# FFN of the last two blocks: one ring of four tiles for the rows of w_down and the columns of w_up

## The chip, the core and the metric

One core of one Trainium2 chip runs the whole program. The metric is the device time of one execution in microseconds (us); the median of three runs is compared. The profile is of one further execution, with its own time.

## What is computed

The reference is one decoder block: dilated attention and a spatial gating unit, then a SwiGLU FFN, on 2048 rows of width 1024, all in float32. Only the end of the program matters here, the FFN:

```
D_FF = 2816
h = rms_norm(x, pre_ffn_norm[l])
f = (jax.nn.silu(h @ w_gate[l]) * (h @ w_up[l])) @ w_down[l]
x = x + rms_norm(f, post_ffn_norm[l])
```

The 2048 rows are four blocks of 512 rows. The FFN of blocks 0 and 1 is done block by block; blocks 2 and 3, "the last two blocks", are done together with seven half-size products in place of eight (Strassen's scheme in Winograd's form).

## The kernel before

A float32 operand is split for TensorE (PE) into a high and a low part: ScalarE (ACT) casts it into `w_hi` (L1055), VectorE (DVE) subtracts to get `w_lo` (L1056), and three matmuls hi·hi, hi·lo, lo·hi take the place of one. `split` does this into a ring of W_SPL = 4 pairs, so the cast of a product waits until the product four places earlier has left PE.

**st_up** (L1136 on, named by its matmuls, L1169) runs NG = 11 rounds, g = 0 to 10, one for each 256 columns of `w_gate` and `w_up`. A round has a gate half and an up half. Each half is the seven products in the order PROD = (1, 2, 5, 6, 3, 7, 4), each of 12 matmuls of 128x512 into one PSUM bank, so a half has 84 matmuls and a round 168. For a half:

- `st_raw` loads two tiles of 512 KB with columns of the weight: the gate's into `raw` (a ring of F_RAW = 4, pool `rw`), the up half's into `rau` (a ring of 2, pool `up`). The left operands of products 1, 2 and 4 are pieces of these tiles; those of 5, 6, 3 and 7 are four sums that GpSimd (POOL) makes into `ss` tiles (L1154 to L1157).
- `gain_b` takes each finished bank out of PSUM into the half's four slots A, B, D and E: copies on ACT (L1065, L1069), additions on DVE (L1067 to L1076) and two more on POOL (L1074, L1077). A and E of the gate half lie in `fe` tiles (pool `us`), B and D and all slots of the up half in `fs` tiles (pool `up`).

Once a round the rows of `w_down` of that round, two tiles of 128x1024, are turned into four combinations in place by DVE (L1175 to L1178) and stored to the DRAM tiles `tS` for the last stage. They have a tile of their own, `wd`, with one buffer. At the end of a round come the silu (L1182), the product gate·up (L1183, four times), POOL's sums into `fc` (L1187 to L1190) and seven stores to `fS`.

```
            wr = pool.tile([P, 2, 1024], F32, name="wd", tag="wd", bufs=1)
            for k in range(2):
                self.dma(wr[:, k], t["w_down"][0, 256 * g + P * k:256 * g + P * k + P])
            for n in range(2):
                r = self.raw0 if g == 0 and n == 0 else self.st_raw(g, n, self.rw if n == 0 else pool)
```

Round 0's gate columns, `raw0`, are loaded ahead, while the FFN of block 1 (`ffn_down(1)`) still runs; pool `rw` is open then. Pool `up` takes memory that `ffn_down(1)` still uses: nothing can be written there before the last of its eight stores `out<-y` (each made ready by a DVE row L907, which waits for a load `xr`) has landed.

All DMAs here stand in the queue of SyncE (SP), in one order, as do the instructions of each engine in theirs; a scheduler fixes these orders when the program is built, from priorities and its own estimates. What stands at the head and waits holds what is behind it. The splits have a raised priority (HP_W = 1000), and so have the rows that empty PSUM (HP_E = 1000).

**st_down**, the last stage, multiplies by `w_down` (L1255); it reads `fS` and `tS`.

Of the kernel before, what the change touches and what calls it, by code (L numbers as in the profile page):

```python
# [10 lines left out]
F32 = mybir.dt.float32  # L11
# [7 lines left out]
P = 128  # L19
# [68 lines left out]
F_RAW = 4  # L88
# [12 lines left out]
class Body:  # L101
# [977 lines left out]
    def st_raw(self, g, n, pool):  # L1079

        w = self.t[("w_gate", "w_up")[n]][0].rearrange("(k p) c -> p k c", p=P)
        r = []
        for j in range(2):
            r.append((pool.tile([P, 1024], F32, name="raw", tag="raw", bufs=F_RAW) if n == 0 else
                      pool.tile([P, 1024], F32, name="rau", tag="rau", bufs=2)).rearrange("p (k c) -> p k c", k=4))
            self.dma(r[j], w[:, 4 * j:4 * j + 4, 256 * g:256 * g + 256])
        return r

    def st_first(self):
        self.raw0 = self.st_raw(0, 0, self.rw)  # L1090

    def st_prep(self, pool):

# [45 lines left out]
    def st_up(self, pool, spool):  # L1139

        nc, t, v, q = self.nc, self.t, self.nc.vector, self.nc.gpsimd

        used = 0
        for g in range(NG):
            both = []
            wr = pool.tile([P, 2, 1024], F32, name="wd", tag="wd", bufs=1)
            for k in range(2):
                self.dma(wr[:, k], t["w_down"][0, 256 * g + P * k:256 * g + P * k + P])
            for n in range(2):
                r = self.raw0 if g == 0 and n == 0 else self.st_raw(g, n, self.rw if n == 0 else pool)  # L1150
                a11, a12, a21, a22 = (r[j][:, :, P * i:P * i + P] for i in range(2) for j in range(2))
                s1, s2, s3, s4 = (spool.tile([P, 4, P], F32, name="ss", tag="ss", bufs=F_SUM) for _ in range(4))
                with self.tc.high_priority(HP_W):
                    q.tensor_tensor(s1, a21, a22, ALU.add)  # L1154
                    q.tensor_tensor(s2, s1, a11, ALU.subtract)
                    q.tensor_tensor(s4, a12, s2, ALU.subtract)
                    q.tensor_tensor(s3, a11, a21, ALU.subtract)  # L1157
                left = {1: a11, 2: a12, 3: s4, 4: a22, 5: s1, 6: s2, 7: s3}
                slots = [spool.tile([P, TB], F32, name="fe", tag="fe", bufs=2) if n == 0 and j in (0, 3) else
                         pool.tile([P, TB], F32, name="fs", tag="fs", bufs=F_OUT) for j in range(4)]  # L1160
                for i in PROD:
                    hi, lo = self.split(left[i])
                    ps = self.psf[used >= 4 and used % 2].tile([P, 512], F32, name="d", tag="d")
                    used += 1
                    for k in range(4):
                        c = slice(k * P, k * P + P)
                        h, l = self.th[i][k]
                        for n, (a, b) in enumerate(((hi, h), (hi, l), (lo, h))):
                            nc.tensor.matmul(ps, a[:, c], b, start=(k == 0 and n == 0), stop=(k == 3 and n == 2))  # L1169
                    self.gain_b(i, ps, lambda n: slots[n])  # L1170
                    yield
                both.append(slots)
                if len(both) == 1:
                    b11, b12, b21, b22 = (wr[:, i, 512 * j:512 * j + 512] for i in range(2) for j in range(2))
                    v.tensor_tensor(b11, b12, b11, ALU.subtract)  # L1175
                    v.tensor_tensor(b12, b22, b12, ALU.subtract)
                    v.tensor_tensor(b22, b22, b11, ALU.subtract)
                    v.tensor_tensor(b21, b21, b22, ALU.subtract)  # L1178
                    for i, b in ((5, b11), (7, b12), (6, b22), (4, b21)):
                        self.dma(self.tS[i][g], b)  # L1180
            for gt, up in zip(*both):
                nc.scalar.activation(gt, gt, AF.Silu)  # L1182
                v.tensor_tensor(up, gt, up, ALU.mult)  # L1183

            a12, a22, a21, a11 = both[1]
            s1, s2, s4 = (pool.tile([P, TB], F32, name="fc", tag="fc", bufs=F_CMB) for _ in range(3))
            q.tensor_tensor(s1, a21, a22, ALU.add)  # L1187
            q.tensor_tensor(s2, s1, a11, ALU.subtract)
            q.tensor_tensor(s4, a12, s2, ALU.subtract)
            q.tensor_tensor(a21, a11, a21, ALU.subtract)  # L1190
            for i, a in ((1, a11), (2, a12), (5, s1), (6, s2), (3, s4), (7, a21), (4, a22)):
                self.dma(self.fS[i][g], a)
            yield
# [235 lines left out]
```

## Time and profile before

| | us |
|---|---|
| median of 3 runs (2467.46 to 2468.42) | 2468.33 |
| the profiled execution, its own time | 2461.28 |
| its span, first to last instruction | 2459.2 |
| PE busy in the span | 2276.9 (93%) |
| DVE, ACT, POOL busy | 1770.4, 1167.9, 358.5 |
| st_up, from its first matmul to its last | 1759.3 to 2230.4 |

The mean granted clock of PE is 0.968 of full speed. Times in the rows count from the span's start; a row of a timeline gives start, duration, engine, line and operation, and in brackets how long the engine was idle before it and what ended that. Starts of pipelined instructions overlap the end of those before.

### The profile page before, as it was taken

Reading aid. Unit: us, or ns where it says so; the run is one execution under the profiler, and the core shown is the slowest. Engines: PE = TensorE matmul, PEld = TensorE weight load, DVE = VectorE, ACT = ScalarE, POOL = GpSimd, SP = SyncE. Lnnn points to the kernel's source line nnn. Section 1 sums busy time; section 2 is a strip of 40 time slices with the busy share of each in tenths; the row PEclk is TensorE's granted clock in tenths of the full one; section 3 lists DMA queues with packets and bytes.
Section 4 is the critical chain, followed back from the end, with each engine's and each line's share of the span. In section 5 each row is a group of like instructions: output and inputs, shape, how many; then the busy total and the mean of one; then the engine's idle time right before and its main releaser. Section 6 shows DMA issues by size and latency. Waiting matters only on the chain. (4 is left out here: it accounts for less than half of the span.)

```text
span 2459.2 us, 32809 instructions
## 1 busy us (share of the span) xinstructions
PE 2276.9 (93%) x10421; PEld 1859.5 (76%) x10421; DVE 1770.4 (72%) x3430; ACT 1167.9 (47%) x2141; POOL 358.5 (15%) x389
## 2 busy tenths in 40 slices
PE   7998869889888899999999999999979999999997
PEld 6776757677676778887777888788757778887886
DVE  5426887986798995868999744668767676675567
ACT  7425765655645653535555533545423233334543
POOL 0001000000000000000000000000054566561012
PEclk9998989999999999999999999999989999999999
DMA  7868667778777655457665435778466533326655
GB/s 243 296 206 270 210 200 220 226 228 239 249 223 233 197 158 153 137 145 228 202 191 160 135 116 166 226 232 263 147 211 225 199 112 108 103 99 227 199 177 197
DMA packets 346748, 476.84 MB, mean 194 GB/s; under 512 B 30768, under 2 KB 174672, under 8 KB 346064
## 3 DMA queue, kind: packets, MB, share of 16 engines
q1 hardware_dynamic: 345296, 470.57, 60.8%
q0 software_dynamic: 1280, 4.20, 0.5%
q8 instruction: 82, 1.34, 0.2%
q14 instruction: 90, 0.74, 0.1%
HBM read 365.12 MB, written 109.52 MB: 193 GB/s over the span
## 5 line engine op out<-in xcount | busy, mean ns | idle before, releaser
L180 DVE TENSOR_TENSOR w_lo<-w_raw,w_hi 128x512 fp32r<-128x512 f32 x368 | 251.8, 687 | 176.9 <-ACT w_hi L179 163.8
L179 ACT CAST w_hi<-w_raw 128x512 fp32r<-128x512 f32 x368 | 227.4, 619 | 314.4 <-PE d L208 241.9
L208 PE MATMUL d<-ah,w_hi 128*128 128x512 f32 x704 | 276.9, 394 | 4.9 <-ACT ah L334 4.9
L208 PE MATMUL d<-al,w_hi 128*128 128x512 f32 x704 | 276.1, 392 | 0.0
L208 PE MATMUL d<-ah,w_lo 128*128 128x512 f32 x704 | 275.5, 391 | 0.0
L1169 PE MATMUL d<-th,w_lo 128*128 128x512 f32 x616 | 246.9, 401 | 20.3 <-DVE w_lo L1056 20.2
L1169 PE MATMUL d<-th,w_hi 128*128 128x512 f32 x616 | 246.7, 400 | 12.7 <-ACT w_hi L1055 12.7
L1169 PE MATMUL d<-tl,w_hi 128*128 128x512 f32 x616 | 244.1, 396 | 0.0
L1056 DVE TENSOR_TENSOR w_lo<-raw,w_hi 128x512 fp32r<-128x512 f32 x187 | 142.6, 801 | 69.4 <-ACT w_hi L1055 67.9
L1055 ACT CAST w_hi<-raw 128x512 fp32r<-128x512 f32 x187 | 106.9, 618 | 133.0 <-PE d L1255 80.4
L208 PE MATMUL d<-w_hi,hh 128*128 128x512 f32 x384 | 155.7, 408 | 8.8 <-DVE io L445 4.5
L208 PE MATMUL d<-w_lo,hh 128*128 128x512 f32 x384 | 156.9, 409 | 4.3 <-DVE w_lo L180 4.3
L1169 PEld LDWEIGHTS d<-th,w_lo 128*128 128x128 f32 x616 | 118.0, 192 | 52.7 <-DVE w_lo L1056 25.9
L208 PEld LDWEIGHTS d<-ah,w_hi 128*128 128x128 f32 x704 | 133.0, 189 | 30.6 <-ACT ah L334 5.2
L208 PE MATMUL d<-w_hi,hl 128*128 128x512 f32 x384 | 154.9, 405 | 0.0
L827 POOL MEMSET ph<- 128x128 f32 x64 | 13.2, 206 | 953.8 <-PE pv L805 531.9
L208 PEld LDWEIGHTS d<-al,w_hi 128*128 128x128 f32 x704 | 132.7, 188 | 25.6
L208 PEld LDWEIGHTS d<-ah,w_lo 128*128 128x128 f32 x704 | 132.4, 188 | 25.8
L1169 PEld LDWEIGHTS d<-th,w_hi 128*128 128x128 f32 x616 | 118.6, 193 | 38.5 <-ACT w_hi L1055 14.0
L208 PE MATMUL d<-w_hi,fh 128*128 128x512 f32 x352 | 139.7, 397 | 1.5 <-ACT fh L1022 1.1
L208 PE MATMUL d<-w_hi,fl 128*128 128x512 f32 x352 | 137.3, 392 | 2.1 <-DVE fl L1023 2.1
L1169 PEld LDWEIGHTS d<-tl,w_hi 128*128 128x128 f32 x616 | 118.4, 192 | 26.1
(285 smaller groups left out, 5606.4 us busy)
## 6 DMA issues: line engine op xcount, KB each, us to landing
w_raw<-in_w_in SPq DMA_DIRECT2D x136, 256.0 KB
w_lo<-wc SPq DMA_DIRECT2D x96, 256.0 KB
w_raw<-in_w_gate SPq DMA_DIRECT2D x88, 256.0 KB
w_raw<-in_w_up SPq DMA_DIRECT2D x88, 256.0 KB
w_raw<-in_w_down SPq DMA_DIRECT2D x88, 256.0 KB
araw<-fD SPq DMA_DIRECT2D x88, 256.0 KB
raw<-fS SPq DMA_DIRECT2D x77, 256.0 KB
w_raw<-in_w_out SPq DMA_DIRECT2D x64, 256.0 KB
```

The costliest lines, as they stand in the source:

```text
L179: nc.scalar.copy(hv, rv)
L180: nc.vector.tensor_tensor(lv, rv, hv.bitcast(F32), ALU.subtract)
L208: nc.tensor.matmul(banks[b], lhsT, rhs, start=(k == 0 and j == 0), stop=(k == nk - 1 and j == len(ops) - 1))
L827: nc.gpsimd.memset(t[:, :o].bitcast(F32), 0.0)
L1055: nc.scalar.copy(hv, src)
L1056: nc.vector.tensor_tensor(lv, src, hv.bitcast(F32), ALU.subtract)
L1169: nc.tensor.matmul(ps, a[:, c], b, start=(k == 0 and n == 0), stop=(k == 3 and n == 2))
```

## The change

The up half's columns and the rows of `w_down` now share one ring of four tiles `rau`, in place of two `rau` and one `wd` of double size: the memory is the same. In round 0 and in odd rounds `w_down` is asked for first, in the other rounds the columns of `w_up`. `st_first` now loads the up columns of round 0 ahead as well; they go into the two `raw` tiles in which, before, the gate columns of round 1 were loaded ahead.

```diff
         r = []
+        tag, bufs = ("raw", F_RAW) if pool is self.rw else ("rau", 4)
         for j in range(2):
-            r.append((pool.tile([P, 1024], F32, name="raw", tag="raw", bufs=F_RAW) if n == 0 else
-                      pool.tile([P, 1024], F32, name="rau", tag="rau", bufs=2)).rearrange("p (k c) -> p k c", k=4))
+            r.append(pool.tile([P, 1024], F32, name=tag, tag=tag, bufs=bufs).rearrange("p (k c) -> p k c", k=4))
             self.dma(r[j], w[:, 4 * j:4 * j + 4, 256 * g:256 * g + 256])
         return r
 
     def st_first(self):
-        self.raw0 = self.st_raw(0, 0, self.rw)
+        self.raw0 = [self.st_raw(0, n, self.rw) for n in range(2)]
...
+        def down(g):
+            w = [pool.tile([P, 1024], F32, name="rau", tag="rau", bufs=4) for _ in range(2)]
+            for k in range(2):
+                self.dma(w[k], t["w_down"][0, 256 * g + P * k:256 * g + P * k + P])
+            return w
+
         used = 0
         for g in range(NG):
             both = []
-            wr = pool.tile([P, 2, 1024], F32, name="wd", tag="wd", bufs=1)
-            for k in range(2):
-                self.dma(wr[:, k], t["w_down"][0, 256 * g + P * k:256 * g + P * k + P])
+            if g == 0:
+                wr, raws = down(g), self.raw0
+            elif g % 2:
+                wr, raws = down(g), [self.st_raw(g, 0, self.rw), self.st_raw(g, 1, pool)]
+            else:
+                raws = [self.st_raw(g, n, p) for n, p in enumerate((self.rw, pool))]
+                wr = down(g)
             for n in range(2):
-                r = self.raw0 if g == 0 and n == 0 else self.st_raw(g, n, self.rw if n == 0 else pool)
+                r = raws[n]
...
-                    b11, b12, b21, b22 = (wr[:, i, 512 * j:512 * j + 512] for i in range(2) for j in range(2))
+                    b11, b12, b21, b22 = (wr[i][:, 512 * j:512 * j + 512] for i in range(2) for j in range(2))
```

The four combinations of `w_down` are L1187 to L1190 in the changed file, its silu L1194, its gate·up L1195.

The scheduler orders the program anew. First place: ACT at the end of round 0's gate half. `raw` and `rau` are weight columns, `ss` POOL's sums, `fs<-d` with L1069 is the copy of slot B out of PSUM. Before:

```order
L1055 CAST w_hi<-raw 128x512
L1069 COPY fs<-d 128x512
L1182 ACTIVATE fs<-fs 128x512 x2
L1182 ACTIVATE fe<-fe 128x512
L1055 CAST w_hi<-rau 128x512 x2
L1055 CAST w_hi<-ss 128x512 x3
```

With the change:

```order
L1055 CAST w_hi<-raw 128x512 x3
L1055 CAST w_hi<-ss 128x512 x3
L1069 COPY fs<-d 128x512
L1065 COPY fs<-d 128x512
L1055 CAST w_hi<-ss 128x512
L1194 ACTIVATE fs<-fs 128x512 x2
```

Five casts of the up half (two of its columns, three of its sums) now stand ahead of the copy that needs pool `up`; before, all seven stood behind it.

Second place: DVE at the start of round 2's gate half. `w_lo<-ss` are the low parts of products 5, 6, 3 and 7, `w_lo<-raw` that of product 4; `wd<-wd` and `rau<-rau` are combinations of `w_down`. Before:

```order
L1183 TENSOR_TENSOR fs<-fs 128x512
L1175 TENSOR_TENSOR wd<-wd 128x512
L1071 TENSOR_TENSOR fs<-d,fs 128x512
L1056 TENSOR_TENSOR w_lo<-ss,w_hi 128x512
L1183 TENSOR_TENSOR fs<-fe,fs 128x512
L1176 TENSOR_TENSOR wd<-wd 128x512
L1177 TENSOR_TENSOR wd<-wd 128x512
L1056 TENSOR_TENSOR w_lo<-ss,w_hi 128x512
L1178 TENSOR_TENSOR wd<-wd 128x512
L1067 TENSOR_TENSOR fe<-d,fe 128x512
```

With the change:

```order
L1195 TENSOR_TENSOR fs<-fe,fs 128x512
L1187 TENSOR_TENSOR rau<-rau 128x512
L1056 TENSOR_TENSOR w_lo<-ss,w_hi 128x512
L1067 TENSOR_TENSOR fe<-d,fe 128x512
L1056 TENSOR_TENSOR w_lo<-ss,w_hi 128x512
L1188 TENSOR_TENSOR rau<-rau 128x512
L1189 TENSOR_TENSOR rau<-rau 128x512
L1056 TENSOR_TENSOR w_lo<-raw,w_hi 128x512
L1190 TENSOR_TENSOR rau<-rau 128x512
```

Of the four combinations one is left ahead of the low part of product 3, and two stand ahead of that of product 4. The even blocks of `w_down` are combined in the up halves instead, and the gate half of round 3 has none.

Third place: SP at the same point of the changed program, with the numbers of the tiles; `tS5_3` is combination 5 of block 3 of `w_down`, `fS3_1` a store of round 1.

```order
L139 DMA tS4_2_274<-rau_18647 128x512
L139 DMA rau_18960<-in_w_down 128x1024
L139 DMA fS4_1_185<-fs_18485 128x512
L139 DMA fS5_1_196<-fc_18624 128x512
L139 DMA fS6_1_207<-fc_18625 128x512
L139 DMA fS7_1_218<-fs_18486 128x512
L139 DMA fS2_1_163<-fs_18484 128x512
L139 DMA fS3_1_174<-fc_18626 128x512
L139 DMA rau_18961<-in_w_down 128x1024
L139 DMA tS5_3_286<-rau_18960 128x512
```

Block 3's second tile of `w_down` is asked for behind the last store of round 1. Before, the queue at this store was ahead with `w_down`:

```order
L139 DMA wd_19599<-in_w_down 128x1024 x2
L139 DMA tS5_5_288<-wd_19599 128x512
L139 DMA fS4_1_185<-fs_18483 128x512
L139 DMA fS5_1_196<-fc_18622 128x512
L139 DMA fS6_1_207<-fc_18623 128x512
```

There the combinations of block 5 were stored ahead of round 1's results; now block 3 follows them.

## Rows read from the trace of the kernel before

**Rows 1.** Stretches: from:to, length, each engine's busy us (instructions), PE's clock, DMA share, GB/s.
```profile
1759.30:1817.10 57.80, 43.08 (x169) 33.87 (x168) 40.92 (x59) 15.57 (x27) 20.07 (x14) 0.85 0.52 173
1817.10:2003.10 186.00, 167.72 (x689) 133.32 (x689) 132.20 (x153) 51.01 (x91) 104.69 (x69) 0.95 0.56 192
2003.10:2230.40 227.30, 227.30 (x995) 186.51 (x994) 151.06 (x168) 75.41 (x131) 134.31 (x89) 1.00 0.31 100
```

**Rows 2.** Waits of PE in st_up: total us, times, the longest.
```profile
PE d L1169 <- DVE w_lo L1056: 20.2, 11, 3.7
PE d L1169 <- ACT w_hi L1055: 12.7, 3, 11.6
```

**Rows 3.** Timeline of PE, round 0, gate half to up half.
```profile
1783.84 0.40 PE L1169 MATMUL d<-th,w_lo 128*128 128x512 f32 x1
1795.84 0.79 PE L1169 MATMUL d<-th,w_hi 128*128 128x512 f32 x1 [11.61 <-ACT w_hi L1055]
1796.44 0.63 PE L1169 MATMUL d<-tl,w_hi 128*128 128x512 f32 x1
...
1800.44 0.40 PE L1169 MATMUL d<-th,w_lo 128*128 128x512 f32 x1
```

**Rows 4.** Timeline of ACT, round 0.
```profile
1788.98 0.59 ACT L1069 COPY fs<-d 128x512 f32<-128x512 f32 x1 [15.03 <-DMA out<-y]
...
1795.17 0.62 ACT L1055 CAST w_hi<-rau 128x512 fp32r<-128x512 f32 x1 [1.41 <-DMA rau<-in_w_up]
...
1808.89 0.62 ACT L1055 CAST w_hi<-raw 128x512 fp32r<-128x512 f32 x1 [1.64 <-PE d L1169]
```

**Rows 5.** Timeline of DVE, round 0: the last two rows L907.
```profile
1783.46 0.75 DVE L907 SCALAR_TENSOR_TENSOR y<-y,po_y,xr 128x512 f32<-128x512 f32 x1 [1.41 <-DMA xr<-x]
1785.93 0.75 DVE L907 SCALAR_TENSOR_TENSOR y<-y,po_y,xr 128x512 f32<-128x512 f32 x1 [1.71 <-DMA xr<-x]
```

**Rows 6.** Timeline of SP's queue, round 0.
```profile
1779.67 7.37 SPq L139 DMA_DIRECT2D out<-y  x4
1788.93 0.81 SPq L139 DMA_DIRECT2D wd<-in_w_down  x2
```

**Rows 7.** Timeline of DVE, gate half of round 2.
```profile
1877.13 1.78 DVE L1177 TENSOR_TENSOR wd<-wd 128x512 f32<-128x512 f32 x1
...
1880.50 1.75 DVE L1056 TENSOR_TENSOR w_lo<-ss,w_hi 128x512 fp32r<-128x512 f32 x1
```

**Rows 8.** Timeline of PE, gate half of round 2.
```profile
1882.30 0.79 PE L1169 MATMUL d<-th,w_lo 128*128 128x512 f32 x1 [3.71 <-DVE w_lo L1056]
```

**Rows 9.** Timeline of SP's queue: the first store fS of two rounds, five rounds apart.
```profile
2003.15 0.34 SPq L139 DMA_DIRECT2D fS<-fs  x1
...
2195.36 0.33 SPq L139 DMA_DIRECT2D fS<-fs  x1
```

**Rows 10.** Timeline of ACT: cast for the gate half's first product, a late round.
```profile
2029.78 0.62 ACT L1055 CAST w_hi<-raw 128x512 fp32r<-128x512 f32 x1 [1.58 <-PE d L1169]
```

**Rows 11.** Timeline of DVE in that gate half: low parts of products 3 and 7.
```profile
2045.00 1.79 DVE L1056 TENSOR_TENSOR w_lo<-ss,w_hi 128x512 fp32r<-128x512 f32 x1
...
2047.31 1.18 DVE L1056 TENSOR_TENSOR w_lo<-ss,w_hi 128x512 fp32r<-128x512 f32 x1
```

**Rows 12.** Timeline of POOL in that gate half.
```profile
2047.90 1.75 POOL L1189 TENSOR_TENSOR fc<-fs,fc 128x512 f32<-128x512 f32 x1
...
2051.43 1.63 POOL L1155 TENSOR_TENSOR ss<-ss,raw 128x512 f32<-128x512 f32 x1
```

**Rows 13.** Timeline of SP's queue in that gate half: last store fS of a round.
```profile
2049.67 0.32 SPq L139 DMA_DIRECT2D fS<-fc  x1
2050.22 0.38 SPq L139 DMA_DIRECT2D raw<-in_w_gate  x1
```

**Rows 14.** Timelines of SP's queue and DVE: a load of w_down and its first reader.
```profile
1947.63 0.81 SPq L139 DMA_DIRECT2D wd<-in_w_down  x2
...
1951.38 0.69 DVE L1175 TENSOR_TENSOR wd<-wd 128x512 f32<-128x512 f32 x1 [0.42 <-DMA wd<-in_w_down]
```

## The prediction

> **What bounds the kernel now.** I looked first at where st_up, the only stage touched, runs below its own best rate. The stretches [rows 1] show three parts: from 2003.1 us on PE is busy all the time at full clock; from 1817.1 to 2003.1 it is busy 167.7 of 186.0 us at a mean clock of 0.95; in round 0, the first 57.8 us, only 43.1 at 0.85. So the last part gives the price of an undisturbed round: five rounds lie between two like stores [rows 9], (2195.36 - 2003.15) / 5 = 38.44 us, which is 2.75 for each of the 14 products. Against that, the stage loses time in its first five rounds alone.
>
> Then the waits of PE [rows 2]: 32.9 us, all on ACT's casts or DVE's low parts; no load of weights is a releaser directly. I split the loss by place.
>
> *Round 0.* The gate half's last matmul starts at 1783.84 and the next at 1795.84 [rows 3]. ACT shows why [rows 4]: it stood 15.03 us at the copy of slot B, in pool `up`, until the last store `out<-y` had landed at 1788.9; the cast of the up columns behind it then waited until 1795.17 for a load that SP could only issue behind those same stores [rows 6]. The cast at 1808.89 [rows 4] was released by the end of the up half's fourth product (the ring of four pairs); three products more give the end of round 0: 1808.89 + 3 x 2.75 = 1817.1. The up half thus took 1817.1 - 1784.1 = 33.0 us in place of 19.2.
>
> *Rounds 1 to 10.* They end at 2230.4 [rows 1], so they took 413.3 us; ten undisturbed ones take 384.4. The loss is 28.9 us, in the four boundaries between rounds 0 and 4, 7.2 each. One of them is shown: DVE does combinations of `w_down` at 1.78 us a row [rows 7], the low part of product 3 comes behind them, and PE waits 3.71 us for it [rows 8]. These boundaries lose because the scheduler lets `w_down` run far ahead: its eleven blocks are done in the first five rounds, as the third place of the order shows.
>
> **The change, part by part.**
>
> *(a) Round 0, the up half.* Its columns are in SBUF long before, and POOL's four sums follow the gate's at once. Product 1 starts where the gate half ends, 1784.1. Product 2 can't: PSUM banks are taken in turn, and its bank is the one that held the gate half's third product, slot B, whose copy still waits for the last `out<-y`. The stores depend on the same L907 rows as before [rows 5]; the low parts that now stand between them fall into DVE's waits for `xr` (1.71 and 1.41 us idle [rows 5], 0.7 a row). New on SP is one gate tile of 512 KB just ahead of the last store. Its buffer is free by then, so it does not block the queue, but its packets do go first: nothing at best, and at worst its own landing, which I bound by the 3.75 us of a 512 KB load (below). Stores and loads overlap, so I take 0.6: the store lands at 1789.5, the copy takes 0.6 [rows 4], product 2 starts at 1790.1. PE has then been idle about 3.3 us and comes back at half clock: before, after its pause, nine matmuls came 0.427 apart in place of 0.228 [rows 3], a price of 1.8 us. Six products: 1790.1 + 6 x 2.75 + 1.8 = 1808.4. **Gain: 1817.1 - 1808.4 = 8.7 us** (5.5 to 9.3 by the bounds).
>
> *(b) `w_down` no longer runs ahead.* With tiles freed only by up columns, block 2 waits for round 1's up half, block 4 for round 3's, and each odd block for the even one before it. Even blocks are combined in up halves, where DVE has idle time; odd ones at the next gate half's start. At the boundary of rounds 0 and 1 the combinations (block 1) stand ahead of POOL's additions, whose results DVE would wait for anyway: I cost them at nothing. The cover is DVE's wait for POOL; without it they cost 4 x 1.78 at most, of which three products of slack (8.2 us) take all. So the loss of rounds 1 to 10 goes, **28.9 us**, but for what follows.
>
> *(c) The odd blocks 3, 5, 7 and 9: a new wait.* Take a late gate half as a clock: the cast for product 1 is released at 2029.78 [rows 10], so product 1 starts three products later, 2038.0, and product 4, the seventh, at 2054.5; its third matmul wants the low part at 2054.95. On DVE one combination (1.78 [rows 7]) now comes before the low part of product 3: that moves from 2046.8 to 2048.5 [rows 11]; PE wants it at 2049.4, so it costs nothing, with 0.9 to spare. Then DVE meets the second combination, which needs block 3's second tile. SP issues that behind the round's last `fS` store; this waits for POOL until 2049.65 [rows 12], and the next load starts at 2050.22 [rows 13]. From issue to first reader a load of this shape took 1951.38 - 1947.63 = 3.75 us [rows 14]. So DVE goes on at 2053.95; two combinations and the low part of product 4 at 0.69 each (a row that meets no POOL work [rows 14]) end at 2056.0, and PE waits 1.05 us. POOL has ended its second sum at 2053.1 [rows 12], and its next row waits for one that stands behind on DVE. Behind DVE's wait are also the low parts for the up half, wanted from 2058 on; they follow in 2 to 3 us. Four boundaries: **loss 4.2 us**.
>
> Here a row bears against me: a combination took 0.69 us [rows 14] in one place and 1.78 in another [rows 7], and a low part 1.75, where POOL was at work. With these, (c) ends at 2053.95 + 2 x 1.78 + 1.75 = 2059.3, a wait of 4.3 us, which also brings the half clock, as after 3.71 us [rows 8], 1.8 more: 24 us in place of 4.2. The Trainium skill has this as a rule (SBUF — State Buffer, Who interferes with whom): GpSimd and a DVE row with two SBUF inputs exclude each other on a shared port pair, and the later one waits. By this rule alone, were POOL busy there, the sum would be the 24. The trace agrees with it on the two durations; it does not say that POOL is at work at that moment, and I take 0.69.
>
> *(d) At nothing.* Gate columns of round 1 now arrive later, with the loads that round 2's had, at 1785, and are wanted at 1800. Later up columns come about a round ahead of use. SP's waits for tiles hold `fS` stores for a few us; no reader wants those before st_down. Bytes, matmuls and the stages before and after are the same.
>
> **The sum.** 8.7 + 28.9 - 4.2 = 33.4 us. The profiled execution would go from 2461.28 to 2427.9. It was 7.05 below the median of the runs, and a gain in waits should carry over: 2468.33 - 33.4 = **2434.9 us**. Its own range: 2428, with (a) at its best, no half clock after the pause (1.8) and no wait in (c); 2445, with (a) at 5.5 and 0.7 us more at each of ten boundaries.
>
> **The rivals.**
>
> 1. *POOL is at work in (c).* The 24 us of above: gain 8.7 + 28.9 - 24 = 13.6, **2454.7**; with two of the three rows slowed, about 2447. For it: a slip of 2 us in POOL's order suffices. Against it: POOL's next row depends on DVE.
> 2. *The stalls move to the odd boundaries.* Each costs what each of the four cost, 7.2 us. Four of them: only (a) is left, **2459.6**; with that of round 0 to 1 as a fifth, gain 1.5, **2466.8**, no change. For it: the same rows remain on the same engine. Against: there were four combinations and the wait for POOL in one place, now two or three.
> 3. *Slower: one combination chain in every round.* Were `w_down` in the way at all ten boundaries at 7.2 us, the loss would be 72: 2468.33 - 37.6 + 72 = **2502.7**. It turns slower when a boundary costs over 37.6 / 10 = 3.8 us. The place would be the low parts of products 3 and 4, the price DVE held by a late tile. For it: a late tile on an in-order engine did hold DVE before. Against: the order leaves the even boundaries without such rows, so odd ones would have to cost over 9 us.
> 4. *The ring does not change places.* It does only in part: block 3 goes into the tiles of block 2, not of the up columns. What I cost is the order as built, so this gives no other time.
>
> **How the numbers follow.** Forecast 0.66, rival 1 0.18 (half of it below 2452), rival 2 0.09 (0.06 and 0.03), rival 3 0.05, nothing seen 0.02. The range 2427 to 2453 takes the forecast and over half of rival 1, and leaves out some 0.2. A measurement of this kernel tells 0.2%, 4.9 us, from no change. Faster by more: 0.66 + 0.18 + 0.06 = 0.90; within: 0.05; slower: 0.05.
>
> **What would show it.** (a) PE: a pause of about 3 us after the twelfth matmul of round 0's up half, ended by the copy of slot B; end of round 0 near 1808. (b) No waits of PE at the boundaries into rounds 1, 2 by more than 2 us and into 3, 5 at all, and full clock from 1815 on. (c) DVE waiting for `rau<-in_w_down` at the second combination of odd blocks, and PE for `w_lo` about 1 us, four times. The forecast is wrong if these four waits are 4 us, if PE waits 2 us or more in even rounds, or if the last `out<-y` lands after 1792.

## The result and the profile after

Four executions of the changed kernel took 2435.27 to 2442.55 us, median 2439.82; four of the kernel before, on the same chip, had a median of 2468.38. The ratio is 0.9882, 95% interval 0.9860 to 0.9905. The forecast was 2434.9, in a range of 2427 to 2453, and faster with a chance of 0.90; the median lies in the range, 4.9 us above the forecast. The parts of the sum came out otherwise than forecast. The profiled execution took 2438.17 us (span 2435.2), and its `st_up` is 25 us shorter, not 33.

What follows goes by the length of `st_up` and its halves: from the first matmul of a half (84 matmuls) to that of the next, in PE's timeline. An undisturbed half is 19.23 us, a round 38.45.

| | `st_up` starts | round 0 | rounds 1 to 10 | `st_up` |
|---|---|---|---|---|
| before | 1759.29 | 57.87 | 413.15 | 471.02 |
| after | 1759.69 | 44.97 | 400.85 | 445.82 |

The stretches of the changed kernel, one line each, with the columns of [rows 1]: round 0; round 1 and the gate half of round 2; up to the gate half of round 8; the rest.

```profile
1759.70:1804.66 44.96, 41.82 (x169) 33.28 (x168) 36.91 (x56) 15.34 (x28) 22.21 (x15) 0.92 0.51 173
1804.66:1874.43 69.77, 61.34 (x254) 48.60 (x252) 48.82 (x54) 17.28 (x31) 41.79 (x28) 0.95 0.56 186
1874.43:2109.38 234.95, 231.57 (x1009) 189.19 (x1008) 169.04 (x193) 75.73 (x132) 147.68 (x96) 1.00 0.47 155
2109.38:2205.51 96.13, 96.13 (x421) 78.92 (x420) 65.41 (x77) 32.98 (x58) 52.26 (x34) 1.00 0.35 118
```

Only the last stretch, five halves of 19.23, is undisturbed. The second should take three such halves, 57.7, and takes 69.8. So of the 28.7 us that rounds 1 to 10 lost before, 16.3 are still lost: 0.35 in the gate half of round 1, 7.39 in its up half (26.62), 4.34 in the gate half of round 2 (23.57), and 1.11, 1.00 and 2.11 in the gate halves of rounds 4, 6 and 8 (20.34, 20.23, 21.34). These are the waits of PE in `st_up`, the answer to [rows 2]; below them DVE's waits for `w_down`, first with the change, then before.

```profile
PE d L1181 <- DVE w_lo L1056: 11.2, 7, 2.1
PE d L1181 <- ACT w_hi L1055: 3.7, 3, 2.6
```

```profile
DVE rau L1188 <- DMA rau<-in_w_down: 22.6, 9, 5.2
...
DVE rau L1187 <- DMA rau<-in_w_down: 17.2, 5, 10.2
```

```profile
DVE wd L1175 <- DMA wd<-in_w_down: 12.7, 6, 3.7
...
DVE wd L1176 <- DMA wd<-in_w_down: 4.2, 4, 2.1
```

PE waits 14.9 us in place of 32.9. DVE, though, stands 39.8 us at combinations (L1187, L1188) whose tile of `w_down` has not landed, in place of 16.9 before. Runs 5 to 7 test how much of what remains comes from these combinations.

*Round 0.* The forecast had PE stop at the second product of the up half until slot B was copied. PE's timeline at the start of the first product and of the fourth:

```profile
1785.21 0.39 PE L1181 MATMUL d<-th,w_lo 128*128 128x512 f32 x1
1785.43 0.39 PE L1181 MATMUL d<-th,w_hi 128*128 128x512 f32 x1
...
1793.67 0.39 PE L1181 MATMUL d<-th,w_hi 128*128 128x512 f32 x1
```

Nothing stops: three products in 8.24 us, 2.75 each, and the half takes 19.23. Yet the copy was even later than forecast (ACT's timeline, then SP's queue):

```profile
1792.62 0.59 ACT L1069 COPY fs<-d 128x512 f32<-128x512 f32 x1 [3.79 <-DMA out<-y]
```

```profile
1783.54 3.60 SPq L139 DMA_DIRECT2D out<-y  x3
1787.24 0.39 SPq L139 DMA_DIRECT2D raw<-in_w_gate  x1
1788.51 0.33 SPq L139 DMA_DIRECT2D out<-y  x1
```

The last store was issued at 1788.51 and landed at 1792.6, not 1789.5; the copy ended at 1793.2. PE did not care: the second product ran before the copy, so slot B's bank is not its bank. The bank goes to the fourth product, which starts at 1793.67, half a microsecond after the copy; in runs 3, 4 and 7 PE does wait for this copy, and at the fourth product each time. Why the banks are given out in this order, no run shows. The same place before is in [rows 3, 4, 6].

*Rounds 1 and 2.* PE's waits there, and DVE in the up half of round 1:

```profile
1832.54 0.50 PE L1181 MATMUL d<-th,w_hi 128*128 128x512 f32 x1 [2.64 <-ACT w_hi L1055]
...
1835.23 0.79 PE L1181 MATMUL d<-th,w_lo 128*128 128x512 f32 x1 [1.96 <-DVE w_lo L1056]
...
1864.14 0.50 PE L1181 MATMUL d<-th,w_lo 128*128 128x512 f32 x1 [1.67 <-DVE w_lo L1056]
...
1872.02 0.50 PE L1181 MATMUL d<-th,w_lo 128*128 128x512 f32 x1 [2.11 <-DVE w_lo L1056]
```

```profile
1833.29 0.69 DVE L1187 TENSOR_TENSOR rau<-rau 128x512 f32<-128x512 f32 x1 [10.20 <-DMA rau<-in_w_down]
1833.89 0.68 DVE L1076 TENSOR_TENSOR fe<-d,fe 128x512 f32<-128x512 f32 x1
1834.49 0.68 DVE L1056 TENSOR_TENSOR w_lo<-ss,w_hi 128x512 fp32r<-128x512 f32 x1
```

DVE stands 10.20 us at the first combination of block 2. Behind it is the low part that PE wants: PE waits 1.96, and ten matmuls follow 0.43 apart (a granted clock of 0.50, the 1.2 GHz level). PE's wait before that, 2.64, is another: it ended at 1832.54, before DVE's did, with a cast of ACT (1831.88) that stood behind a silu. Both waits and the slow matmuls come to 7.4 us. The silu on ACT, and POOL:

```profile
1831.35 0.63 ACT L1194 ACTIVATE fs<-fs 128x512 f32<-128x512 f32 x1 [11.78 <-POOL fs L1074]
```

```profile
1822.50 1.74 POOL L1169 TENSOR_TENSOR ss<-rau 128x512 f32<-128x512 f32 x1
...
1827.43 1.30 POOL L1166 TENSOR_TENSOR ss<-raw 128x512 f32<-128x512 f32 x1 [3.20 <-issue]
```

The silu waits for POOL's L1074 (1830.05), and POOL does that row behind its sums of round 2's gate columns, which it begins only at 1827.43. The trace does not name what ended that wait, but the second of the two tiles of columns was issued 4.7 us earlier, at 1822.74, and in runs 5 and 10 POOL begins there 4.7 and 4.9 us after the same load. SP had stood until 1820.8 at a store `fS` of POOL's L1201; the load heads these rows of SP:

```profile
1822.74 0.51 SPq L139 DMA_DIRECT2D raw<-in_w_gate  x1
1823.30 2.48 SPq L139 DMA_DIRECT2D rau<-in_w_up  x2
1825.88 0.45 SPq L139 DMA_DIRECT2D raw<-in_w_gate  x1
1826.43 0.44 SPq L139 DMA_DIRECT2D rau<-in_w_down  x1
```

Before, when round 0's up columns took none of the `raw` tiles, the same tile was issued at 1774.70. The tile of `w_down` is late by POOL and SP too: block 2 goes into a tile of round 1's up columns, and POOL's last sum reads that until 1824.24. SP reaches the load at 1826.43, behind four others, and it lands at 1833.3, 6.9 us later.

*A later boundary* (gate half of round 4), on DVE, SP, POOL and PE:

```profile
1938.57 1.78 DVE L1187 TENSOR_TENSOR rau<-rau 128x512 f32<-128x512 f32 x1
1940.28 1.78 DVE L1056 TENSOR_TENSOR w_lo<-ss,w_hi 128x512 fp32r<-128x512 f32 x1
...
1947.97 0.69 DVE L1188 TENSOR_TENSOR rau<-rau 128x512 f32<-128x512 f32 x1 [4.21 <-DMA rau<-in_w_down]
1948.70 0.69 DVE L1189 TENSOR_TENSOR rau<-rau 128x512 f32<-128x512 f32 x1
1949.31 0.68 DVE L1056 TENSOR_TENSOR w_lo<-raw,w_hi 128x512 fp32r<-128x512 f32 x1
```

```profile
1943.24 0.32 SPq L139 DMA_DIRECT2D fS<-fc  x1
1943.61 0.42 SPq L139 DMA_DIRECT2D rau<-in_w_down  x1
```

```profile
1938.06 1.75 POOL L1202 TENSOR_TENSOR fs<-fs 128x512 f32<-128x512 f32 x1
...
1945.01 1.29 POOL L1167 TENSOR_TENSOR ss<-ss,raw 128x512 f32<-128x512 f32 x1
1952.53 1.63 POOL L1074 TENSOR_TENSOR fs<-fs 128x512 f32<-128x512 f32 x1 [6.23 <-DVE fs L1073]
```

```profile
1950.05 0.50 PE L1181 MATMUL d<-th,w_lo 128*128 128x512 f32 x1 [0.84 <-DVE w_lo L1056]
```

This is step (c) as it was forecast, row by row: the second tile issued behind the last `fS` store, DVE at L1188 until it lands (4.4 us after its issue), POOL with nothing to do from 1946.3 to 1952.5, combinations and low part at 0.69, and PE waiting 0.84 where 1.05 was forecast.

### The profile page after: what moved, and what is told of

Its sections match the earlier page's. It is cut to its first block, busy times and chain, and to the rows that moved or that the text cites. A ratio compares the mean times of both kernels' runs of the same rounds, so it can differ in the third digit from the quotient of the medians.

```text
span 2435.2 us, 32794 instructions
## 1 busy us (share of the span) xinstructions
PE 2268.8 (93%) x10421; PEld 1857.9 (76%) x10421; DVE 1766.2 (73%) x3430; ACT 1168.5 (48%) x2141; POOL 364.3 (15%) x389
## 5 line engine op out<-in xcount | busy, mean ns | idle before, releaser
L1181 PEld LDWEIGHTS d<-th,w_lo 128*128 128x128 f32 x616 | 117.0, 190 | 39.5 <-DVE w_lo L1056 14.6
L208 PE MATMUL d<-w_lo,fh 128*128 128x512 f32 x352 | 137.5, 391 | 0.0
```

Source lines behind the costliest of these rows:

```text
L208: nc.tensor.matmul(banks[b], lhsT, rhs, start=(k == 0 and j == 0), stop=(k == nk - 1 and j == len(ops) - 1))
```

## The experiments

Every kernel ran beside the kernel before on one chip; the ratio is to that kernel's runs beside it. Lengths of `st_up` are taken as above.

### 1. Only the early load

The kernel before, with:

```diff
-            r.append((pool.tile([P, 1024], F32, name="raw", tag="raw", bufs=F_RAW) if n == 0 else
+            r.append((pool.tile([P, 1024], F32, name="raw", tag="raw", bufs=F_RAW) if pool is self.rw else
...
-        self.raw0 = self.st_raw(0, 0, self.rw)
+        self.raw0 = [self.st_raw(0, n, self.rw) for n in range(2)]
...
-                r = self.raw0 if g == 0 and n == 0 else self.st_raw(g, n, self.rw if n == 0 else pool)
+                r = self.raw0[n] if g == 0 else self.st_raw(g, n, self.rw if n == 0 else pool)
```

> Only the early load of round 0's up columns; w_down keeps its own single tile and the up columns their two, as before. My theory (the two parts add): round 0 takes 45.0 us as in the changed kernel in place of 57.9, PE has no pause at the start of its up half, and rounds 1 to 10 keep a loss of about 29 us, since w_down runs ahead as before. Time about 12.9 below the kernel before, 2455. Rival A (the parts don't add): with round 0 shorter the same rows of w_down are squeezed into fewer rounds, the loss of rounds 1 to 10 grows to 35 or more, and the gain is under 7, 2462 or more. Rival B (the ring gives nothing): the early load alone gives all, 2440.

Measured: 2460.21 us, ratio 0.9963 (0.9946 to 0.9980). Round 0 took 44.88 us, rounds 1 to 10 420.15; `st_up` is 6.0 shorter than before. Rival A holds by the stage (the median is 2 us under its number): the early load gives its 13 us in round 0 and gives back 7.0 in rounds 1 to 10, where the loss is now 35.7. Their gate halves of rounds 1 to 4 take 26.64, 29.19, 27.57 and 28.61.

### 2. Only the ring

The changed kernel, with:

```diff
-        self.raw0 = [self.st_raw(0, n, self.rw) for n in range(2)]
+        self.raw0 = self.st_raw(0, 0, self.rw)
...
-                wr, raws = down(g), self.raw0
+                raws = [self.raw0, self.st_raw(g, 1, pool)]
+                wr = down(g)
```

> Only the ring: round 0's up columns are not loaded ahead, they take two tiles of the ring first, and w_down of block 0 the other two. My theory (the two parts add): PE pauses 10 to 12 us between the halves of round 0, which takes 57 to 58 us as before, and rounds 1 to 10 lose 12 to 17 us in place of 29, most of it in the up half of round 1 and the gate half of round 2. Gain 11 to 16, 2452 to 2457. Rival: the ring's own loss in rounds 1 and 2 comes from round 0 being short; with the pause back it goes, rounds 1 to 10 lose only the 4 us of the odd blocks, gain about 25, 2443.

Measured: 2449.21 us, ratio 0.9922 (0.9896 to 0.9947). The two stretches of this kernel, round 0 and rounds 1 to 10:

```profile
1777.71:1835.11 57.40, 43.82 (x170) 34.09 (x168) 41.05 (x56) 15.46 (x27) 20.88 (x14) 0.85 0.48 163
1835.11:2232.38 397.27, 388.42 (x1682) 315.76 (x1680) 285.76 (x323) 125.83 (x221) 242.63 (x158) 1.00 0.45 149
```

My theory held for the stage's numbers: the pause of round 0 is back (10.28 us), rounds 1 to 10 lose 12.8, and `st_up` is 16.4 shorter than before. The median is 3 us under its range. The place was a miss: the up half of round 1 takes 19.23 and loses nothing, and the loss is in the gate halves of rounds 1 and 2 (24.25 and 23.27). So the 7.4 us of the changed kernel's up half came with the early load, as the rival had it, and others came in their stead. The parts don't simply add: 6.0 + 16.4 = 22.4, both together 25.2. The early load costs 7.0 us of new waits without the ring, and 3.6 with it (400.85 - 397.27).

### 3. Round 1 takes its up columns first

```diff
-            elif g % 2:
+            elif g % 2 and g > 1:
```

> The changed kernel, but round 1 takes its up columns from the ring before w_down of block 1. In the changed kernel DVE stood 10.20 us at the first combination of block 2, PE lost 7.4 us in the up half of round 1 and 4.3 in the gate half of round 2. My theory (a chain in the ring: up columns of round 1 wait for the stores of block 0, POOL's sums wait for these columns, block 2 is loaded into tiles that POOL frees, and DVE stands in order behind it): with the columns first, POOL's sums of round 1's up half end before 1820 in place of 1824.2, DVE's wait for block 2 falls under 5 us and PE's loss in that half under 2.5; time 5 to 9 below the changed kernel, 2431 to 2435. Rival (DVE and POOL slow each other, whatever the ring does): the sums still end after 1822, the wait stays at 8 to 11 us, time within 2 of the changed kernel.

Measured: 2445.63 us, ratio 0.9902 (0.9870 to 0.9935); `st_up` 446.57. The mechanism was right where I looked: POOL's sums of round 1's up half ended 59.5 us after the stage's start in place of 64.6, DVE's wait for block 2 fell from 10.20 to 6.29 (more than expected still), and the up half of round 1 took 19.23. The length of the stage was the rival's, 0.8 us from the changed kernel (the medians are 5.8 apart, with intervals that overlap), for another reason: the gate half of round 1 now took 26.41, that of round 2 24.91. DVE and PE in the gate half of round 1:

```profile
1824.04 1.78 DVE L1188 TENSOR_TENSOR rau<-rau 128x512 f32<-128x512 f32 x1
1825.86 1.63 DVE L1189 TENSOR_TENSOR rau<-rau 128x512 f32<-128x512 f32 x1
1827.41 1.75 DVE L1056 TENSOR_TENSOR w_lo<-ss,w_hi 128x512 fp32r<-128x512 f32 x1
```

```profile
1822.48 0.50 PE L1181 MATMUL d<-th,w_lo 128*128 128x512 f32 x1 [1.49 <-DVE w_lo L1056]
...
1829.21 0.79 PE L1181 MATMUL d<-th,w_lo 128*128 128x512 f32 x1 [3.70 <-DVE w_lo L1056]
```

Block 1's combinations now stand among the low parts of the gate half, with POOL at work: 26.41 - 19.23 = 7.2 us, the price of a boundary in the kernel before, with its 3.71 us wait [rows 7, 8].

### 4. Every round takes its up columns first

```diff
-            elif g % 2:
+            elif g < 0:
```

> The changed kernel, but every round after round 0 takes the up columns first and w_down second, odd rounds too. My theory: as in the run before this one for rounds 1 and 2, and the waits of DVE for the second tile of blocks 3, 5, 7 and 9 (4.0 to 5.2 us each, issued behind the last store fS3) go to places where a half round of slack lies ahead; PE's waits of 0.84, 0.71 and 1.83 us in the gate halves of rounds 4, 6 and 8 go as well. Another 4 to 8 below the run before, 2424 to 2430. Rival 1: a block of w_down is then late in every round, as block 2 was in the changed kernel, PE loses 2 us or more in each of eight rounds, and the time is 2450 or more. Rival 2: nothing but the place of the waits changes, within 2 of the run before.

Measured: 2442.0 us, ratio 0.9888 (0.9865 to 0.9912); `st_up` 447.75. A miss: the gate half of round 1 lost 8.6 us, and the gate halves of rounds 3 to 10 all lose something now, 0.9 to 2.2 us each. By the stage it is rival 2, 1.2 us from run 3; the medians are 3.6 apart, with intervals that overlap. Asking for tiles in another order moves the late combination; it does not remove it.

### 5. No combinations

```diff
-                    v.tensor_tensor(b11, b12, b11, ALU.subtract)
-                    v.tensor_tensor(b12, b22, b12, ALU.subtract)
-                    v.tensor_tensor(b22, b22, b11, ALU.subtract)
-                    v.tensor_tensor(b21, b21, b22, ALU.subtract)
```

> The changed kernel without the 44 combinations of w_down on DVE: the blocks are stored as they were loaded. The loads, the ring and the stores stay. My theory (what is left of the loss in the changed kernel, 16.3 us in rounds 1 to 10, is DVE standing at a combination for a late tile, and combinations standing between low parts): rounds 1 to 10 take 384.5 to 387, each gate half 19.2, the up half of round 1 as well; st_up takes 430 to 432 in place of 445.8. Rival (the loss comes from POOL's sums and the loads of the columns, DVE only waits with the rest): the up half of round 1 still takes over 23 us and rounds 1 to 10 over 394.

Measured, one execution: 2431.48 us, `st_up` 430.99, rounds 1 to 10 386.68. From round 1 on all gate halves take 19.2, as my theory has it; the up half of round 1 is still longer than it says, 21.37. So 14.2 of the 16.3 us hang on the combinations, with loads, stores and ring in place; 2.1 are the other chain of round 1, from the late gate tile over POOL and ACT: PE waits 1.53 us there, for ACT's cast.

### 6. Odd blocks combined in their own round

`self.low` is the low part just made. `issue_after` queues the rows that it holds behind the instruction named, on the same engine.

```diff
-            nc.vector.tensor_tensor(lv, src, hv.bitcast(F32), ALU.subtract)
+            self.low = nc.vector.tensor_tensor(lv, src, hv.bitcast(F32), ALU.subtract)
...
                     self.gain_b(i, ps, lambda n: slots[n])
+                    if both and i == PROD[2] and g % 2 and g > 1:
+                        b11, b12, b21, b22 = (wr[k][:, 512 * j:512 * j + 512] for k in range(2) for j in range(2))
+                        with self.tc.issue_after(self.low.ins):
+                            v.tensor_tensor(b11, b12, b11, ALU.subtract)
+                            v.tensor_tensor(b12, b22, b12, ALU.subtract)
+                            v.tensor_tensor(b22, b22, b11, ALU.subtract)
+                            v.tensor_tensor(b21, b21, b22, ALU.subtract)
+                        for k, b in ((5, b11), (7, b12), (6, b22), (4, b21)):
+                            self.dma(self.tS[k][g], b)
                     yield
...
-                if len(both) == 1:
+                if len(both) == 1 and not (g % 2 and g > 1):
```

> The changed kernel, but the combinations of blocks 3, 5, 7 and 9 are queued on DVE behind the low part of the third product of their own round's up half, no longer at a gate half's start a round earlier; all else stays. The gate halves of rounds 2, 4, 6 and 8 took 23.57, 20.34, 20.23 and 21.34 us. My theory (those four lose 8.5 us by DVE standing at the second combination for a tile, and by one combination of 1.78 among the low parts): all four take 19.2 to 19.4 and the up half of round 1 stays at 26 to 27; st_up 437 to 438. Rival (POOL's work slows DVE there with or without combinations): gate half of round 2 over 21, the others over 20.

Measured: 2435.97 us, ratio 0.9874 (0.9852 to 0.9896); `st_up` 442.91. Neither number: the gate halves of rounds 2, 4, 6 and 8 took 20.05, 20.49, 20.51 and 20.66, a loss of 4.8 in place of 8.6, and that of round 10, undisturbed before, took 20.48. DVE and PE around the gate half of round 4, where no odd block stands any more:

```profile
1927.21 0.69 DVE L1197 TENSOR_TENSOR rau<-rau 128x512 f32<-128x512 f32 x1 [2.49 <-DMA rau<-in_w_down]
```

```profile
1938.15 0.50 PE L1181 MATMUL d<-th,w_lo 128*128 128x512 f32 x1 [0.34 <-DVE w_lo L1056]
...
1941.54 0.50 PE L1181 MATMUL d<-th,w_lo 128*128 128x512 f32 x1 [0.36 <-DVE w_lo L1056]
```

The even block, a round ahead of its use, is now what holds DVE: 2.49 us for its second tile, at the end of an up half. DVE enters the next half late and meets POOL's work there (rows of 1.77 us). That this makes PE's small waits is read from the order of the rows; run 7, which moves the even blocks too, is the test. I had counted the waits of even blocks as free.

### 7. Every block combined in its own round

As in 6, for every `g`, and the old place of the combinations is gone; the difference to 6:

```diff
-                    if both and i == PROD[2] and g % 2 and g > 1:
+                    if both and i == PROD[2]:
...
-                if len(both) == 1 and not (g % 2 and g > 1):
...
```

> The changed kernel, but the combinations of every block are queued on DVE behind the low part of the third product of their own round's up half. The order in which the ring's tiles are asked for stays. My theory: no combination stands at a boundary any more and each block has half a round more to land, so rounds 1 to 10 take 385 to 388 in place of 400.9, the up half of round 1 under 20; st_up 430 to 434, time 12 to 16 below the changed kernel, 2424 to 2428. Rival 1 (the tiles come free later too, since w_down holds them longer): up columns or w_down are late in each round, PE loses 1.5 us or more in most up halves and rounds 1 to 10 take over 400. Rival 2: the loss in round 1 stays, since its up columns wait in the ring behind block 0's stores: its up half 24 or more.

Measured: 2425.25 us, ratio 0.9829 (0.9804 to 0.9854). Its two stretches:

```profile
1769.39:1815.08 45.69, 41.16 (x169) 32.45 (x168) 37.30 (x55) 15.22 (x28) 21.95 (x15) 0.96 0.50 169
1815.08:2199.63 384.55, 384.55 (x1682) 315.44 (x1680) 290.89 (x323) 125.90 (x221) 242.93 (x158) 1.00 0.48 158
```

My theory holds, to its edge: PE is busy for all of the 384.55 us of rounds 1 to 10, each half 19.22 to 19.24, and DVE has no wait for a tile of `w_down`. `st_up` takes 430.24, 15.6 below the changed kernel, the same as 14.6 by the medians. DVE's combinations take as long as before (the second 1.67, the others 0.69); they only stand where half a round of slack lies ahead. This is also the run that shows what slot B does:

```profile
1803.35 0.59 ACT L1069 COPY fs<-d 128x512 f32<-128x512 f32 x1 [5.81 <-DMA out<-y]
```

```profile
1803.99 0.50 PE L1181 MATMUL d<-th,w_hi 128*128 128x512 f32 x1 [1.42 <-ACT fs L1069]
```

Its up half began at 1794.16, so the fourth product was due at 1802.4; here the copy came after that, and PE waited for it, 1.42 us. The mechanism of step (a) exists, two products later than I had put it.

### 8. The same, up columns first in every round

```diff
-            elif g % 2:
+            elif g < 0:
```

> As the run before this one, and every round takes the up columns from the ring before w_down. My theory: the order of asking no longer matters once the combinations stand in their own round; st_up within 1.5 us of the run before. Rival: block 1 asked for last is late for the up half of round 1, or the columns of round 1 come sooner and take 2 us or more off round 1, whichever; st_up differs by over 1.5 us.

Measured: 2434.36 us, ratio 0.9860 (0.9826 to 0.9893); `st_up` 430.80, 0.6 above run 7. The theory holds for the stage. The gate half of round 1 took 2.1 us more than 19.2, and round 0 1.5 less. The medians are 9 us apart with the stage equal and with intervals that overlap; no trace places these 9 us.

### 9. Own round without the ring

Run 1 with the lines of 7, and the views of its one double tile:

```diff
+                        b11, b12, b21, b22 = (wr[:, k, 512 * j:512 * j + 512] for k in range(2) for j in range(2))
```

> The buffers of the kernel before (two tiles for the up columns, one double tile for w_down), with round 0's up columns loaded ahead, and the combinations of every block queued on DVE behind the low part of the third product of their own round's up half. Theory A (what counts is that w_down doesn't run ahead, the ring is only one way to hold it): rounds 1 to 10 take 384.5 to 388, as in the run with the ring, in place of 420 with the early load alone; st_up 430 to 434, time 2424 to 2429. Theory B (the ring itself counts: one double tile of w_down must be emptied by its stores before the next load, so blocks come late): PE loses 1 us or more in the up half of most rounds, rounds 1 to 10 take over 395.

Measured: 2429.34 us, ratio 0.9845 (0.9812 to 0.9877); `st_up` 435.13. Between the two theories:

```profile
1807.17:2197.84 390.67, 387.75 (x1681) 314.58 (x1680) 284.81 (x323) 124.23 (x221) 240.05 (x158) 1.00 0.45 156
```

390.67 is 29.5 below run 1, so the place of the combinations does nearly all of it, with the buffers of the kernel before. The ring is worth 6.1 more, but not as theory B had it: the up halves are all clean, and the gate halves lose 0.15 to 1.6 each.

### 10, 11. The changed kernel and run 7 again, on one chip

No edit to either.

> The changed kernel once more, beside the others on one chip. My theory: st_up takes 445 to 447 us again, with the same long halves (up half of round 1 near 26.6, gate half of round 2 near 23.6), while the start of st_up differs by some us from one execution to the next; that spread, in stages that the change doesn't touch, is why 28.6 by the medians and 25.2 by the stage are the same gain. Rival: the long halves differ from execution to execution by 3 us or more, and the gain isn't settled to that.

> The version with every block combined in its own round, once more, beside the changed kernel on one chip: st_up 430 to 431 us again; time 12 to 18 below the changed kernel of the run before this one. Were the earlier difference of 14.6 by the medians chance, the two would be within 5.

Measured: 2437.63 us, ratio 0.9895 (0.9860 to 0.9930), `st_up` 444.61 with halves of 26.71 and 23.30 where the first profile had 26.62 and 23.57; and 2425.35 us, ratio 0.9821 (0.9802 to 0.9840), `st_up` 428.88. They are 12.3 apart by the medians, 15.7 by the stage. The long halves repeat to 0.3 us, and the difference of the two kernels is not chance; run 7's stage came out 1.4 us shorter than the first time, all of it in round 0, whose up half took 19.53. Both stages lie a little under the ranges that I gave (by 0.4 and 1.1).

### 12. The kernel before again

No edit.

> The kernel before once more, for a second profile. The gain is 28.6 us by the medians, 25.2 by the length of st_up in one profile of each kernel (471.02 and 445.82), and the changed kernel's second profile had 444.61. Theory A (st_up is the same in each execution to about 1.5 us, and the rest of the difference is spread in other stages): st_up 469.5 to 472.5 again, whatever the whole run takes. Theory B (the first profile fell on a short st_up): 474 or more, and the stage's gain is nearer 29.

Measured: 2467.55 us, ratio 0.9996 (0.9977 to 1.0016); `st_up` 470.17. Theory A. The stage's gain is (471.02 + 470.17 - 445.82 - 444.61) / 2 = 25.4 us, inside the interval of the ratio (23.4 to 34.6 us). What is over in the 28.6 of the medians is not settled to a stage; its size is no surprise, as `st_up` started at 1759.29 in one profile of the kernel before and at 1769.27 in the other.

The medians below are from several chips, on which the kernel before took 2466.7 to 2469.5.

| kernel | round 0 | rounds 1 to 10 | `st_up` | median, us |
|---|---|---|---|---|
| before | 57.87 | 413.15 | 471.02 | 2468.4 |
| early load alone | 44.88 | 420.15 | 465.03 | 2460.2 |
| ring alone | 57.40 | 397.27 | 454.67 | 2449.2 |
| both (the change) | 44.97 | 400.85 | 445.82 | 2439.8 |
| early load, own round, no ring | 44.46 | 390.67 | 435.13 | 2429.3 |
| the change, own round | 45.69 | 384.55 | 430.24 | 2425.3 |

## Why the prediction was right, and where it was not

The direction and the size of the whole came out because round 0 and the first rounds were read rightly as the two places with something to gain: 12.9 and 12.3 us were gained there. By steps, against the 33.4 of the sum:

**(a), 8.7 forecast, 12.9 measured.** The step that failed is "its bank is the one that held the gate half's third product": that is so for the up half's fourth product, not for the second. A second error, the store's landing at 1789.5 (it was 1792.6, issued behind the gate tile and after a later last row L907), would have made it worse, and was hidden by the first: PE's fourth product came 0.5 us after the copy. No pause, so no half clock either.

**(b), 28.9 forecast, 21.0 measured.** The loss of 28.7 did go from where it was, but 7.7 us came back in round 1. The step that failed is "even blocks are combined in up halves, where DVE has idle time". Idle time covers work; it does not cover a wait in an in-order queue. I priced the four rows and not the lateness of their tile, though I had the chain (POOL's sum, the store, the load) in hand for the odd blocks. By run 5 this is 5.2 of the up half's 7.4 (26.62 - 21.37); the rest belongs to (d). That block 1 cost nothing at the boundary into round 1 (0.35) was right.

**(c), 4.2 forecast, 8.6 measured.** The mechanism was right to the row, and rounds 4, 6 and 8 together lost 4.2. The term was mis-sized at block 3, in the gate half of round 2: 4.3 in place of 1.05. "It costs nothing, with 0.9 to spare" had DVE on time at the half's start; after block 2 it was not, and the low part of product 3 cost 1.67 of waiting by itself, the second tile 2.11 more. In the other three rounds even blocks were nearly on time (DVE waits 0.57 to 0.73 us for their second tile); the 2.5 us of run 6 came with its own edit.

**(d), at nothing**, failed in one term: "Gate columns of round 1 now arrive later". Those of round 2 do too, and the second of these tiles, issued at 1822.74 in place of 1774.70, held POOL, then ACT, then PE, 2.64 us in the changed kernel. With (b)'s combinations gone (run 5) this chain still costs 2.1. Otherwise (d) held: `st_down` and the stages before did not change, by anything that two executions of one kernel don't show as well.

Sum: 12.9 + 21.0 - 8.6 = 25.3. The stage missed by 8 us, and it missed by no more only because the error of (a) went the other way from those of (b) and (c). That the median came within 5 us is luck besides: the medians are 28.6 apart, 3 more than `st_up` became shorter, and nothing in the forecast gives these 3.

**Rival 1** (POOL at work in (c)) did not come: POOL waited at that moment, and the rows took 0.69. (Its "about 2447" for two slowed rows does not follow from its rows: four waits of 3.25 give 2443.7, and with 1.8 of half clock each 2450.9.) Its mechanism is real elsewhere in the same lines: a combination beside POOL's L1202 took 1.78. The rule of the Trainium skill (SBUF — State Buffer, Who interferes with whom), that GpSimd and a DVE row with two SBUF inputs exclude each other, agrees with both. **Rival 2** was half right in its place (gate halves after odd blocks) and wrong in its price: 1.0 to 4.3, not 7.2. (7.2 was a mean: the gate halves of rounds 1 to 4 of the kernel before lost 9.7, 7.1, 8.5 and 3.2.) **Rival 3** did not come; run 4 is the nearest to it, 0.9 to 2.2 a round. **Rival 4** gave no time of its own.

Of what was to show the steps: the pause of 3 us did not appear; the clock was not full from 1815 on; PE did wait 2 us in the gate half of round 2, and the store did land after 1792, both named as signs of a wrong forecast. No wait fell at the boundaries into rounds 3 and 5, and DVE's wait at L1188 was where it was to be.

## What to carry to other kernels

On an engine that works in order, a row costs what stands behind it while it waits for its data, not its duration; for every row whose input is loaded late, follow the chain that frees the buffer, and count that time even where the engine has idle time enough. A buffer shared to hold back an eager scheduler is a blunt throttle: it stopped `w_down` from running five rounds ahead and left it running one round ahead, and late again and again. Queuing the rows behind a named row of their own round took the stage down by another 15.6 us, and did most of it without the ring. Judge such a change by the length of its own stage: the stages ahead of it moved by 10 us between two executions of one kernel.

## What the runs showed that I had not expected

A load of 512 KB of `w_down` took 6.9 us from issue to its reader when four others were issued in the 4 us ahead of it, and 4.4 when no other load went just ahead of it; I had used 3.75 for all. The core's DMA engines were busy throughout the first stretch and moved 366 GB/s, in the second they were busy for 0.83 of it and moved 238.

The same wait of PE gave stretches at the lower clock of different length. In the gate half of round 0 PE waits 0.4, 0.6 and 2.04 to 2.07 us in all fourteen profiles. Here are the last of these in the changed kernel and in run 7:

```profile
1769.74 0.79 PE L1181 MATMUL d<-th,w_lo 128*128 128x512 f32 x1 [2.05 <-DVE w_lo L1056]
```

```profile
1779.41 0.50 PE L1181 MATMUL d<-th,w_lo 128*128 128x512 f32 x1 [2.05 <-DVE w_lo L1056]
```

Matmuls of 0.63 us at the 1.2 GHz level follow in both, eleven in the first and seven in the second; the half took 25.74 and 24.77. Four of the profiles have ten or eleven, ten have six to eight. I found nothing in the rows ahead of the wait that tells the two apart, so 0.9 us of round 0 is open.
